# The convolution's last four gate and value outputs computed context first, with its transforms, norm and SiLU placed between the latents' outputs, and the second pointwise product started before the convolution has ended

## The chip, the cores and the metric

One core of one Trainium2 chip runs the whole program. The metric is the device time in microseconds (us) from start to end of one execution; the median of several runs is compared. Before the change three runs took 1692.59, 1693.88 and 1698.11 us, so the median is 1693.88 us.

The core has a matrix engine (PE, whose weight loads are listed as PEld), a vector engine (DVE), an activation engine (ACT), a general engine (POOL) and queues that start transfers (SP). Each engine works through its own rows in a fixed order; a row that waits holds up all rows behind it on that engine.

## The reference

Two streams of 256 tokens with 1024 channels, context and latents, go through two layers. The change lies in the first half of layer 0, the convolution module, which runs once for each stream with the same weights:

```python
def conformer_conv(u, rows, w_pw1, b_pw1, w_dw, b_dw, ln_g, ln_b, w_pw2, b_pw2):
    a = u @ w_pw1 + b_pw1
    a = a[..., :CONV_DIM] * jax.nn.sigmoid(a[..., CONV_DIM:])
    ...
        a = dwconv(a, w_dw)
    ...
    a = jax.nn.silu(layer_norm(a + b_dw, ln_g, ln_b))
    return a @ w_pw2 + b_pw2

y = conformer_conv(modulate(h, sh1, sc1), ...)
h = layer_norm(ALPHA * h + g1 * y, ln1_g[i], ln1_b[i])
```

The scales, shifts and gates (`sh1`, `g1`, `sh2` and so on) come from one product of a small vector with `ada_w` for each stream. After the convolution both streams go through a squared-ReLU MLP, and then through layer 1, which neither the change nor its neighbourhood touches.

## The kernel before, in words

Both streams are held as one array of 512 columns, channels on partitions: columns 0 to 255 (`LO`, s = 0) are the context, columns 256 to 511 (`HI`, s = 1) the latents. All products are float32 split into a high and a low part, so each 128x128 block of weights costs three matmuls (`mm3`: L177, L180, L181). The raw weights come by DMA (`raw_load`), ACT rounds them (`wh`, L154), DVE subtracts (`wl`, L155). Four pairs of `wh`/`wl` are held at a time (`NW`).

**First product (pw1).** It has 16 outputs of 128 channels, alternately gate and value, eight channel blocks f in all. Four of them are computed while the inputs arrive. The other twelve, called outputs 0 to 11 here, follow: 0 to 9 over all 512 columns (`gemm_steps(pw1, range(5), ...)`), 10 and 11 in two halves of 256 columns (`pw1_part`). `pw1_epi` applies sigmoid to the gate (ACT L652), multiplies with the value (DVE L655), transposes the block on PE (L658) and copies it to `A`, tokens on partitions (ACT L659). `pw1_next` also steps the adaLN columns of g1 and sc2 on DVE (`ada0.step`, L379, 1.2 us each and two for a step), and after output 5 scales x by ALPHA and adds gate times bias, 16 DVE operations (L768).

**The convolution.** `spectral(h, tt)` does it by a transform for half h of the channels and 128 tokens tt (0 and 1 are the context, 2 and 3 the latents): forward matmuls (L675 for context, L680 for latents), four multiplications by the taps' transform on DVE (L690, L691), inverse matmuls (L701), the bias (DVE L708) and the statistics (L709). Half 0 runs after output 4, half 1 at the end.

**The end of the convolution.** `token_norm(t0)` turns the statistics of two token tiles into scales by a chain of 13 tiny DVE operations (L714 to L719) and then normalizes four tiles on ACT (L723). `silu(s)` takes one stream's normalized tokens back to channels: for each block f two transposes on PE (L743), a sigmoid and an affine on ACT (L746, L747), a product on DVE (L748), and the split into high and low (L154, L155). Two blocks f share one PSUM bank `ln` of which there are two, and two SBUF buffers `S` are rotated through. `ada_sh` computes the columns of sh2 with the matmuls L319 and the fold L327; it uses the one PSUM bank `fl`.

**Second product (pw2).** `gemm2_steps` runs the context's eight outputs, then the latents' eight; it gives back control after the first ko = 4 outputs together and then after each output, and at each return the loop takes two blocks of `silu(1)`. `pw2_epi` adds to x and feeds the layer norm (`Norm`); after output 7 of a stream it calls `ln1_half`, which finishes the norm and writes the MLP's input: DVE L493, L494 and L516, ACT L515, eight times.

**Order.** The program is recorded in the order of the Python code; a scheduler then places each engine's rows, and rows under `pin[0] = True` keep the order of the code. What stands where is fixed before the program runs.

Of the kernel before, what the change touches and what calls it, by code (L numbers as in the profile page):

```python
# [72 lines left out]
def hybrid_kernel(ctx: ExitStack, tc: tile.TileContext, xT, vecs_d, rows_d, wdw_d, ada0_w, ada_w, adar_w, wg_d, pw1a, pw1, pw2, w1_0, w2_0,  # L73
# [335 lines left out]
    class Norm:  # L409
# [3 lines left out]
        def __init__(self, n, bufs):  # L413
            self.n, self.ts, self.i = n, [], 0
            self.acc, self.k, self.s2 = bufs
# [90 lines left out]
    def norm_pair(make):  # L506

        b = [make() for _ in range(3)]
        return [Norm(C, [t[:, sl] for t in b]) for sl in (LO, HI)]
# [20 lines left out]
    cb = xp.tile([P, 2 * D], F32, tag="hl", name="cb").rearrange("p (s c) -> p s c", s=2)  # L530
    padp = open_pool("pads")
# [205 lines left out]
    def silu(s):  # L737
        for f in range(DT):
# [3 lines left out]
            for i in range(2):  # L742
                nc.tensor.transpose(xn[:, i * P:(i + 1) * P], Y[2 * s + i][f // 4][:, f % 4 * P:f % 4 * P + P], ident)  # L743
# [10 lines left out]
    ada0, ada_sh = AdaRows(0, (2, 4)), Ada(6, 2)  # L754
    gb = con.tile([P, 2, DT], F32, name="gb")

    def pw1_next(m, ps):
# [5 lines left out]
        ada0.step((1, 2, 1, 2, 2, 2, 2, 2, 1, 1)[m])  # L763
        if m == 5:
            for s, sl in HALVES:
                nc.vector.tensor_tensor(gb[:, s, :], ad(0, s, "g1"), VA("b_pw2"), op=ALU.mult)
                for f in range(DT):
                    nc.vector.tensor_scalar(x[f][:, sl], x[f][:, sl], ALPHA, gb[:, s, f:f + 1], op0=ALU.mult, op1=ALU.add)  # L768
# [4 lines left out]
    steps = gemm_steps(pw1, range(5), u, T, pw1_next)  # L773
# [53 lines left out]
    raw = raw_load(pw1[5, 0])  # L827
    wl2 = [split_w(raw[:, m * D:(m + 1) * D]) for m in range(2)]
    ps2 = [psum() for _ in range(2)]

    def pw1_part(m, s, kts=range(DT)):
        sl = HALVES[s][1]
        for kt in kts:
            mm3(ps2[m][:, sl], *kcol(wl2[m], kt), *[t_[:, sl] for t_ in u[kt]], kt == 0, kt == DT - 1)

    def part_epi(m, s):
        pw1_epi(10 + m + KO0, ps2[m], 2 * s, 2 * s + 2)
# [12 lines left out]
    next(sp[0])  # L850
    pw1_part(1, 1, range(4))
    next(sp[1])
    pw1_part(1, 1, range(4, DT))
    for _ in sp[0]:
        pass
    part_epi(1, 1)
    for _ in sp[1]:
        pass
    normed = token_norm(0)
    pre_pw2(1)  # L860
    for tt in (2, 3):
# [3 lines left out]
        for _ in sp1:  # L865
            pass
# [901 lines left out]
```

## Time and profile before

| | |
|---|---|
| median of three runs | 1693.88 us |
| the profiled execution | 1694.68 us |
| its span, first to last instruction | 1693.0 us |
| PE busy | 1661.1 us (98%) |
| DVE busy | 1092.0 us (65%) |
| ACT busy | 745.7 us (44%) |
| end of the convolution and both pw2 passes | 129 to 225 us of the span |

The difference between the profiled execution and its span, 1.68 us, lies ahead of the first and behind the last instruction. A row of the timeline gives the start in us from the start of the span, the duration, the engine, the line, and the tiles that are written and read; the bracket at its end is the idle time ahead of it and what ended that. Durations of back to back rows overlap by about a tenth of a microsecond or more, so what an operation costs in a dense run is read from the distance between two starts.

### The profile page before, as it was taken

The numbers are of one execution on the slowest core, as the hardware profiler recorded it, in microseconds if no ns is written. First come the engines' busy times: TensorE is split into PE (matmuls) and PEld (weight loads), VectorE is DVE, ScalarE is ACT, GpSimd is POOL, SyncE is SP. The second block draws the span as 40 slices with busy tenths as digits, with TensorE's granted clock in tenths as the row PEclk, the third lists the DMA queues.
The fourth block names the chain that finished last, engine by engine and source line by source line (L and its number), as shares of the span: only waits on it lengthen the run. The fifth ranks groups of instructions, "written<-read, shape, count | busy, mean of one in ns | idle before, by whom it ended". The sixth has DMA issues, their size and how long they took to land.

```text
span 1693.0 us, 22721 instructions
## 1 busy us (share of the span) xinstructions
PE 1661.1 (98%) x8853; PEld 1366.3 (81%) x8853; DVE 1092.0 (65%) x1964; ACT 745.7 (44%) x1206; POOL 33.4 (2%) x84
## 2 busy tenths in 40 slices
PE   8998999999999999999999999999999999999998
PEld 5754997888888998876688899888877878888886
DVE  7995897876666776763132543453387786678765
ACT  3322763232324465542232532442376674555652
POOL 0000000000000000000000000000011110000000
PEclk9999999999999999999999999999999999999999
DMA  9534216565554054568653642344355555645651
GB/s 386 210 130 160 102 57 225 199 222 199 199 195 178 26 183 158 190 217 274 239 191 101 219 150 100 104 171 144 119 187 198 187 188 212 242 172 218 240 186 47
DMA packets 60668, 301.60 MB, mean 178 GB/s; under 512 B 6066, under 2 KB 20946, under 8 KB 27152
## 3 DMA queue, kind: packets, MB, share of 16 engines
q1 hardware_dynamic: 42832, 285.44, 46.7%
q10 hardware_dynamic: 17728, 14.70, 2.7%
q8 instruction: 70, 1.15, 0.3%
q14 instruction: 38, 0.31, 0.1%
HBM read 284.37 MB, written 15.75 MB: 177 GB/s over the span
## 4 chain that ended last, share of the span: by engine, by line
PE 91%; DVE 5%; ACT 2%; issue 1%; DMA 1%; POOL 0%; SPq 0%; DVEq 0%; ACTq 0%; POOLq 0%
PE mm L177 17%; PE mm L180 17%; PE mm L181 17%; PE mm L192 4%; PE mm L187 3%; PE mm L185 3%; PE mm L1591 3%; PE mm L186 3%; PE mm L196 2%; PE cv L187 2%; PE cv L186 2%; PE cv L185 2%; PE mm L1592 2%; DVE wl L155 1%; PE fl L812 1%; PE ln L177 1%
## 5 line engine op out<-in xcount | busy, mean ns | idle before, releaser
L155 DVE TENSOR_TENSOR wl<-raw,wh 128x1024 fp32r<-128x1024 f32 x346 | 421.8, 1223 | 306.4 <-ACT wh L154 303.3
L154 ACT CAST wh<-raw 128x1024 fp32r<-128x1024 f32 x346 | 360.4, 1050 | 483.4 <-PE mm L180 286.3
L180 PE MATMUL mm<-u,wh 128*128 128x512 f32 (+1 forms) x848 | 301.8, 357 | 1.0 <-DVE u L525 0.6
L177 PE MATMUL mm<-u,wh 128*128 128x512 f32 (+1 forms) x720 | 253.6, 355 | 3.8 <-DVE E L1014 3.2
L181 PE MATMUL mm<-u,wl 128*128 128x512 f32 (+1 forms) x720 | 250.5, 350 | 0.5 <-DVE wl L155 0.5
L180 PEld LDWEIGHTS mm<-u,wh 128*128 128x128 f32 x848 | 161.1, 190 | 24.5 <-issue 1.8
L177 PEld LDWEIGHTS mm<-u,wh 128*128 128x128 f32 x720 | 136.1, 190 | 28.5 <-issue 5.1
L181 PEld LDWEIGHTS mm<-u,wl 128*128 128x128 f32 x720 | 136.8, 190 | 19.9 <-issue 1.4
L177 PE MATMUL mm<-xm,wh 128*128 128x512 f32 x256 | 102.8, 402 | 0.0
L185 PE MATMUL mm<-wh,xl 128*128 128x512 f32 x256 | 101.3, 397 | 0.7 <-ACT wh L154 0.5
L186 PE MATMUL mm<-wh,xl 128*128 128x512 f32 x256 | 100.4, 392 | 0.6 <-DVE xl L155 0.6
L181 PE MATMUL mm<-xm,wl 128*128 128x512 f32 x256 | 100.3, 392 | 0.0
L187 PE MATMUL mm<-wl,xl 128*128 128x512 f32 x256 | 99.6, 394 | 0.3 <-DVE wl L155 0.2
L379 DVE CUSTOM_DVE_ANT_0 raw<-raw,cb,vecs 128x1024 f32<-128x1024 f32 x64 | 81.6, 1281 | 24.1 <-DMA raw<-adar_w 23.6
L177 PE MATMUL mm<-hid,wh 128*128 128x512 f32 (+1 forms) x256 | 93.2, 364 | 0.0
L180 PE MATMUL mm<-hid,wh 128*128 128x512 f32 (+1 forms) x256 | 92.8, 363 | 0.0
L181 PE MATMUL mm<-hid,wl 128*128 128x512 f32 (+1 forms) x256 | 92.8, 363 | 0.0
L1591 PE MATMUL mm<-x,wh 128*128 128x512 f32 x224 | 78.9, 397 | 0.0
L180 PE MATMUL mm<-qq,wh 128*128 128x272 f32 x256 | 73.9, 289 | 0.0
L181 PE MATMUL mm<-qq,wl 128*128 128x272 f32 x256 | 73.5, 288 | 0.0
L177 PE MATMUL mm<-qq,wh 128*128 128x272 f32 x256 | 73.5, 288 | 0.0
L192 PE MATMUL mm<-u,wh 128*128 128x512 f32 x192 | 68.4, 398 | 0.0
(496 smaller groups left out, 3269.8 us busy)
## 6 DMA issues: line engine op xcount, KB each, us to landing
raw<-w SPq DMA_DIRECT2D x64, 1024.0 KB, 4.9
raw<-adar_w SPq DMA_DIRECT2D x32, 1024.0 KB, 4.9
raw<-wo SPq DMA_DIRECT2D x32, 1024.0 KB, 4.8
raw<-ada_w SPq DMA_DIRECT2D x16, 1024.0 KB, 7.2
raw<-wv SPq DMA_DIRECT2D x16, 1024.0 KB, 5.7
raw<-wqT SPq DMA_DIRECT2D x16, 1024.0 KB, 5.5
raw<-wq SPq DMA_DIRECT2D x16, 1024.0 KB, 4.9
raw<-wk SPq DMA_DIRECT2D x16, 1024.0 KB, 4.9
```

Source lines behind the costliest of these rows:

```text
L154: c = nc.scalar.copy(hi, src)
L155: nc.vector.tensor_tensor(lo, src, hi.bitcast(F32), op=ALU.subtract)
L177: a = nc.tensor.matmul(ps, wh, xh, start=start, stop=False)
L180: nc.tensor.matmul(ps, wh, xl, start=False, stop=False)
L181: nc.tensor.matmul(ps, wl, xh, start=False, stop=stop)
L185: nc.tensor.matmul(ps, xh, wh, start=start, stop=False)
L186: nc.tensor.matmul(ps, xl, wh, start=False, stop=False)
L187: nc.tensor.matmul(ps, xh, wl, start=False, stop=stop)
L192: nc.tensor.matmul(ps, wh, x, start=start, stop=stop)
L196: nc.tensor.matmul(ps[:, :C], wl, x[:, :C], start=False, stop=False)
L379: nc.vector.tensor_tensor_reduce(dump, w, cb[:, s, :], 1.0, vecs[:, o:o + 1], ALU.mult, ALU.add, accum_out=ada[self.l][:, m, s:s + 1])
L1591: a = lambda stop: nc.tensor.matmul(ps, wh, u2[kt], start=kt == 0, stop=stop)
```

## The change

- Outputs 8 and 9 are taken out of the full width loop, so outputs 8 to 11 run in halves: the context's four halves first, then the latents' four.
- The context's transforms of half 1 stand between the latents' outputs 9, 10 and 11; `token_norm(0)` and the first three blocks of `silu(0)` are recorded ahead of the epilogue of output 11.
- The sh2 columns are computed in two parts (`Ada(6, 1)`, `Ada(7, 1)`), and the latents' transforms tt = 2 and 3 come between and behind the rest of `silu(0)`.
- pw2 starts with ko = 3 outputs, ahead of the last inverse transform. `token_norm(2)` follows that. A second `next(steps2)` runs output 3 before the loop that takes the blocks of `silu(1)`.
- The 16 operations that scale x move from DVE to ACT, after output 6; the steps of `ada0` are spread differently.
- The norm's sum `acc` gets a pool of its own, since pw2 now starts before the convolution's pool is closed.

```diff
-    ada0, ada_sh = AdaRows(0, (2, 4)), Ada(6, 2)
+    ada0, ada_sh = AdaRows(0, (2, 4)), [Ada(6, 1), Ada(7, 1)]
...
-        ada0.step((1, 2, 1, 2, 2, 2, 2, 2, 1, 1)[m])
-        if m == 5:
+        ada0.step(1 if m % 2 == 0 else 2)
+        if m == 6:
...
-                    nc.vector.tensor_scalar(x[f][:, sl], x[f][:, sl], ALPHA, gb[:, s, f:f + 1], op0=ALU.mult, op1=ALU.add)
+                    nc.scalar.activation(x[f][:, sl], x[f][:, sl], AF.Identity, scale=ALPHA, bias=gb[:, s, f:f + 1])
...
-    steps = gemm_steps(pw1, range(5), u, T, pw1_next)
+    steps = gemm_steps(pw1, range(4), u, T, pw1_next)
...
-    for m in range(2):
-        pw1_part(m, 0)
-        if m == 0:
-            part_epi(0, 0)
-    pw1_part(0, 1, range(4))
-    part_epi(1, 0)
-    pw1_part(0, 1, range(4, DT))
-    part_epi(0, 1)
+    for m in range(8, 12):
+        pw1_part(m, 0, first4)
+        if m == 10:
+            part_epi(9, 0)
+        pw1_part(m, 0, last4)
+        if m != 9 and m != 11:
+            part_epi(m, 0)
+        ada0.step()
+    pw1_part(8, 1, first4)
+    part_epi(11, 0)
+    pw1_part(8, 1, last4)
+    part_epi(8, 1)
+    sp = [spectral(1, tt, banks=("cv", "fl")) for tt in range(4)]
+    next(sp[0])
+    pw1_part(9, 1)
     pre_pw2(0)
-    sp = [spectral(1, tt, banks=("mm", "fl")) for tt in range(2)]
-    next(sp[0])
-    pw1_part(1, 1, range(4))
     next(sp[1])
-    pw1_part(1, 1, range(4, DT))
-    for _ in sp[0]:
-        pass
-    part_epi(1, 1)
-    for _ in sp[1]:
-        pass
-    normed = token_norm(0)
+    pw1_part(10, 1, first4)
+    part_epi(9, 1)
+    pw1_part(10, 1, last4)
+    part_epi(10, 1)
+    run(sp[0])
+    pw1_part(11, 1, first4)
+    run(sp[1])
+    token_norm(0)
+    pw1_part(11, 1, last4)
+    s0 = silu(0)
+    for _ in range(3):
+        next(s0)
+    part_epi(11, 1)
     pre_pw2(1)
-    for tt in (2, 3):
-        sp1 = spectral(1, tt, normed)
-        next(sp1)
-        ada_sh.mm()
-        for _ in sp1:
-            pass
-    ada_sh.end()
-    pin[0] = False
-    for _ in silu(0):
-        pass
-    token_norm(2)
...
+    ada_sh[0].mm()
+    next(sp[2])
+    run(s0)
+    run(sp[2])
+    ada_sh[0].end()
+    next(sp[3])
...
+    steps2 = gemm2_steps(pw2, range(4), sact, HALVES, pw2_epi, lambda dt: hidden[0](dt), ko=3, pre=pre2)
+    next(steps2)
+    ada_sh[1].mm()
+    run(sp[3])
+    ada_sh[1].end()
+    token_norm(2)
+    pin[0] = False
+    next(steps2)
...
     side = silu(1)
-    for _ in gemm2_steps(pw2, range(4), sact, HALVES, pw2_epi, HD, ko=4, pre=pre2):
+    for _ in steps2:
         for _ in range(Z.nsilu):
             next(side, None)
```

Three places show how rows move. The same code stands 4 to 26 lines further down in the changed file: L756 is the transpose of `silu` that was L743, L759 and L760 are its sigmoid and affine (L746, L747), L761 its product (L748), L668 and L671 the product and the transpose of `pw1_epi` (L655, L658), L693 and L714 the latents' forward and the inverse transforms (L680, L701), L722 and L727 the statistics and their sum (L709, L714), L503 and on the chain of `rsqrt` (L499), L527 is the affine of `ln1_half` on ACT (L515). Numbers in the names tell buffers apart.

The first place is DVE at the context's token statistics. Before, `u_558` and `u_560` are the two tokens tiles of half 1, and `mw` is the small tile of the norm's chain:

```order
L708 TENSOR_TENSOR u_558<-cv_1272,bdw 128x512
L155 TENSOR_TENSOR wl_1319<-raw_1312,wh_1318 128x1024
L709 BN_STATS bst<-u_558 128x6
L708 TENSOR_TENSOR u_560<-cv_1284,bdw 128x512
L714 BN_AGGR mv_1291<-bst 128x2
L709 BN_STATS bst<-u_560 128x6
L714 BN_AGGR mv_1291<-bst 128x2
L499 TENSOR_SCALAR mw_1294<-mv_1291 128x2
L500 TENSOR_SCALAR mw_1294<-mw_1294 128x2
L502 TENSOR_TENSOR mw_1294<-mw_1294 128x2
```

In the change the same tiles are `u_561` and `u_563`; `E_1148` is the block of output 11 of the latents, `wl_1407` the low part of pw2's fourth weight block:

```order
L721 TENSOR_TENSOR u_563<-cv_1326,bdw 128x512
L727 BN_AGGR mv_1333<-bst 128x2
L722 BN_STATS bst<-u_563 128x6
L668 SCALAR_TENSOR_TENSOR E_1148<-mm_1313,vecs,E_1148 128x256
L727 BN_AGGR mv_1333<-bst 128x2
L503 TENSOR_SCALAR mw_1336<-mv_1333 128x2
L155 TENSOR_TENSOR wl_1407<-raw_1400,wh_1406 128x1024
L504 TENSOR_SCALAR mw_1336<-mw_1336 128x2
L506 TENSOR_TENSOR mw_1336<-mw_1336 128x2
L507 SCALAR_TENSOR_TENSOR mw_1336<-mw_1336 128x2
```

The product that ends output 11 and the split of a weight block now stand inside the chain of the context's norm; before, one weight split stood ahead of the statistics and nothing inside the chain.

The second place is PE behind that norm. Before, the context's first transposes come behind the forward transform of tile 2 and half of the sh2 product, and write two banks, `ln_1393` and `ln_1412`, in turn:

```order
L680 MATMUL mm_1323<-A,tab 128x512
L680 MATMUL mm_1322<-A,tab 128x512
L319 MATMUL fl_1334<-raw_1335,cs 32x512 x4
L319 MATMUL fl_1334<-raw_1337,cs 32x512 x4
L743 MATMUL ln_1393<-ident,u_557 128x128
L743 MATMUL ln_1412<-ident,u_557 128x128
L743 MATMUL ln_1393<-ident,u_559 128x128
L743 MATMUL ln_1412<-ident,u_559 128x128
```

In the change they come straight behind the last matmuls of output 11 (`mm_1313`):

```order
L181 MATMUL mm_1313<-u_508,wl_1116 128x256
L756 MATMUL ln_1366<-ident,u_560 128x128
L756 MATMUL ln_1366<-ident,u_562 128x128
L756 MATMUL ln_1366<-ident,u_560 128x128
L756 MATMUL ln_1366<-ident,u_562 128x128
L756 MATMUL ln_1385<-ident,u_560 128x128
L756 MATMUL ln_1385<-ident,u_562 128x128
L671 MATMUL ln_1396<-ident,E_1148 128x128 x2
L319 MATMUL fl_1410<-raw_1411,cs 32x512 x4
L319 MATMUL fl_1410<-raw_1413,cs 32x512 x4
L693 MATMUL fl_1426<-A,tab 128x512
L693 MATMUL cv_1425<-A,tab 128x512
```

Four transposes now write one bank (`ln_1366`) in a row, the transposes of output 11 (`ln_1396`) stand behind six of them, and the sh2 product and the forward transform of tile 2, which stood ahead of the transposes, stand behind them all. Behind these rows come the other transposes, the fold, the inverse transform of tile 2, and only then pw2's first row.

The third place is ACT at the latents' `silu` and the context's `ln1_half`. Before, `S_1809` and `S_1818` are the last two blocks of the latents, and L475 is the square root of the context's layer norm:

```order
L746 ACTIVATE S_1809<-ln_1806,vecs 128x256
L747 ACTIVATE S_1809<-ln_1806,vecs 128x256
L746 ACTIVATE S_1818<-ln_1806,vecs 128x256
L747 ACTIVATE S_1818<-ln_1806,vecs 128x256
L453 ACTIVATE L_1803<-x_415 128x256
L154 CAST u_1813<-S_1809 128x256
L154 CAST u_1822<-S_1818 128x256
L154 CAST wh_2294<-raw_2292 128x1024
L453 ACTIVATE L_1861<-x_467 128x256
L154 CAST wh_2298<-raw_2292 128x1024
L475 ACT_TABLE_LOAD
L475 ACTIVATE lc_1872<-lc_1872,eps 128x2
```

In the change the sixth block of the latents (`S_1867`) is the last one ahead of that square root (L479), and the context's affine operations begin:

```order
L759 ACTIVATE S_1867<-ln_1855,vecs 128x256
L760 ACTIVATE S_1867<-ln_1855,vecs 128x256
L154 CAST u_1871<-S_1867 128x256
L479 ACT_TABLE_LOAD
L479 ACTIVATE lc_1921<-lc_1921,eps 128x2
L527 ACTIVATE u_1945<-x_146,cb_1936,ca_1935 128x256
L527 ACTIVATE S_1947<-x_146,cb_1936,ca_1935 128x256
L527 ACTIVATE S_1955<-x_180,cb_1936,ca_1935 128x256
```

The seventh and eighth block (`S_2010`, `S_2019`) stand behind the last of the 16 affine operations:

```order
L527 ACTIVATE u_1993<-x_418,cb_1936,ca_1935 128x256
L527 ACTIVATE u_2001<-x_470,cb_1936,ca_1935 128x256
L527 ACTIVATE S_2003<-x_470,cb_1936,ca_1935 128x256
L759 ACT_TABLE_LOAD
L759 ACTIVATE S_2010<-ln_2007,vecs 128x256
L760 ACTIVATE S_2010<-ln_2007,vecs 128x256
L154 CAST u_2014<-S_2010 128x256
L759 ACTIVATE S_2019<-ln_2007,vecs 128x256
L760 ACTIVATE S_2019<-ln_2007,vecs 128x256
L154 CAST u_2023<-S_2019 128x256
```

The code records `ln1_half` at output 7, and with output 3 taken ahead of the loop only six of the eight blocks are recorded by then, where before all eight were. On PE the matmuls that read `u_2014` and `u_2023` stand ahead of output 3 of the latents and of all that follows.

More of the change, by code (lines that the diff above doesn't have):

```diff
@@ L826, in hybrid_kernel, with pw1_part @@
         pass
[L827 to L831, printed above, removed]
+    late_w = {}
+    def pw1_part(m, s, kts=range(DT), bank=None):
         sl = HALVES[s][1]
+        if kts[0] == 0:
+            late_p[m, s] = psum()
+        if m not in late_w:
+            raw = raw_load(pw1[m // 2, 0])
+            for i in range(2):
+                late_w[m + i] = split_w(raw[:, i * D:(i + 1) * D])
@@ L846, in hybrid_kernel, with run @@
-    pw1_part(0, 1, range(4, DT))
-    part_epi(0, 1)
+        pw1_epi(m + KO0, late_p[m, s], 2 * s, 2 * s + 2)
+    def run(g):
+        for _ in g:
+            pass
+    first4, last4 = range(4), range(4, DT)
+    pin[0] = True
+    for m in range(8, 12):
[8 more added lines that the diff above has]
+    part_epi(11, 0)
```

41 lines of the change are left out of this document (28 added, 13 removed).

## The prediction

> **What bounds the kernel now.** Read first the busy time and the chain of work that ended last, on the page of the profile:
>
> ```profile
> PE 1661.1 (98%) x8853; PEld 1366.3 (81%) x8853; DVE 1092.0 (65%) x1964; ACT 745.7 (44%) x1206; POOL 33.4 (2%) x84
> ...
> PE 91%; DVE 5%; ACT 2%; issue 1%; DMA 1%; POOL 0%; SPq 0%; DVEq 0%; ACTq 0%; POOLq 0%
> ```
>
> PE works 98% of the span and carries 91% of the chain. DVE (65%) and ACT (44%) set the end only where PE waits, so the change is worth what it does to PE's idle time and clock. Then the timeline of PE where the change lies (start, duration, operation; the bracket is the idle time ahead and what ended it):
>
> ```profile
> 105.86 0.50 PE L181 MATMUL mm<-u,wl 128*128 128x512 f32 x1 [0.47 <-DVE wl L155]
> ...
> 130.58 0.63 PE L658 MATMUL ln<-ident,E 128*128 128x128 f32 x4 [0.94 <-ACT wh L154]
> ...
> 152.33 1.13 PE L680 MATMUL mm<-A,tab 64*128 64x512 f32 x4
> 153.39 1.92 PE L319 MATMUL fl<-raw,cs 128*32 128x512 f32 x16
> 158.37 1.39 PE L743 MATMUL ln<-ident,u 128*128 128x128 f32 x4 [3.06 <-ACT u L723]
> 159.69 3.68 PE L701 MATMUL cv<-F,tab 128*64 128x512 f32 x8
> ...
> 164.89 1.93 PE L319 MATMUL fl<-raw,cs 128*32 128x512 f32 x16
> 166.75 0.44 PE L743 MATMUL ln<-ident,u 128*128 128x128 f32 x2
> 167.53 1.94 PE L701 MATMUL cv<-F,tab 128*64 128x512 f32 x8 [0.34 <-DVE F L690]
> 169.40 1.05 PE L327 MATMUL fl<-fold,F 128*128 128x4 f32 x8
> ...
> 171.64 0.38 PE L180 MATMUL mm<-u,wh 128*128 128x256 f32 x1 [0.45 <-DVE u L155]
> ```
>
> PE waits 0.94, 3.06, 0.34 and 0.45 us at the convolution's end, and 0.47 earlier. The large wait ends when ACT has normalized the context. The table of stretches (width, busy time of PE, PEld, DVE, ACT and POOL, granted clock, DMA) shows what comes with it:
>
> ```profile
> 156.00:160.00 4.00, 1.61 (x6) 0.87 (x8) 3.61 (x12) 2.49 (x4) 0.00 (x0) 0.70 0.98 373
> 160.00:164.00 4.00, 4.00 (x10) 0.98 (x8) 1.00 (x2) 1.34 (x3) 0.00 (x0) 0.50 0.59 246
> 164.00:168.00 4.00, 3.66 (x24) 0.81 (x22) 3.12 (x7) 0.78 (x2) 0.00 (x0) 0.95 0.21 35
> ```
>
> The clock is at half for 0.60 x 4.0 = 2.4, 4.0 and 0.10 x 4.0 = 0.4 us, 6.8 in all, about 157.6 to 164.4. PE has work again from 158.37, so 6.0 us run at half and 3.0 are lost. The most that a perfect cover of this stage could win is thus 4.8 us of waits and 3.0 of clock, under 0.5%.
>
> **The change part by part**, against the profiled 1694.68.
>
> *x is scaled on ACT.* What leaves DVE, what ACT pays, and where:
>
> ```profile
> L768 DVE TENSOR_SCALAR x<-x,gb 128x256 f32<-128x256 f32 x16 | 4.7, 345 | 0.0
> ...
> L515 ACT ACTIVATE u<-x,cb,ca 128x256 fp32r<-128x256 f32 x16 | 9.4, 590 | 1.3 <-DVE x L494 1.3
> ...
> 105.42 0.58 ACT L659 COPY A<-ln 128x512 f32<-128x512 f32 x1 [23.63 <-PE ln L658]
> ```
>
> 16 operations of 0.345, busy 4.7 us with their overlaps, leave DVE. The nearest ACT rows, an affine operation of the same size, take 0.59; 16 are 9.4 us, beside ACT's 23.63 idle us ahead of 105.42. No row shows this very operation on ACT; the ends are 0 (covered) and +9.4 (all in PE's path). I take 0, by the idle row. DVE, freed, ends the weight split earlier: the wait of 0.47 goes, **−0.5**. Should the cover fail, the copy at 105.42 is the next on ACT that something waits for. The end of 9.4 is left out of the range, since 9.4 fits twice into 23.63.
>
> *Outputs 8 and 9 in halves.* 48 matmuls of 512 columns become 96 of 256:
>
> ```profile
> 126.99 0.39 PE L180 MATMUL mm<-u,wh 128*128 128x512 f32 x1
> 127.22 0.39 PE L181 MATMUL mm<-u,wl 128*128 128x512 f32 x1
> ...
> 171.86 0.28 PE L181 MATMUL mm<-u,wl 128*128 128x256 f32 x1
> 171.98 0.28 PE L180 MATMUL mm<-u,wh 128*128 128x256 f32 x1
> ```
>
> Starts lie 0.23 apart at 512 and 0.12 at 256: 96 x 0.12 − 48 x 0.23 = **+0.5**. SP issues the same weight loads in nearly the same order; DMA in the quoted stretches is at most 0.98 full in one and 0.21 in another, and none of PE's waits above ends on a DMA. I take 0 for the loads. The step of `ada0` and the separate pool for `acc` add no instruction; 0.
>
> *Waits that go.* The four waits from 130.58 to 171.64 belong to an order that no longer exists: −4.8, and with the clock −3.0, **−7.8**. What is late in their place comes now.
>
> *Transposes right behind their producers.* Output 7's transposes, and later L491, stand with no matmuls between product and transpose. Neither wait is in the trace; the ends are 0 and twice the 0.94 of the 130.58 row. I take 0.9 each, **+1.8**, near that row.
>
> *The first hole.* The rows of DVE in the statistics chain, and ACT's and the epilogue's:
>
> ```profile
> 137.08 0.48 DVE L655 SCALAR_TENSOR_TENSOR E<-mm,vecs,E 128x256 f32<-128x256 f32 x1 [5.32 <-PE mm L181]
> ...
> 151.52 1.22 DVE L155 TENSOR_TENSOR wl<-raw,wh 128x1024 fp32r<-128x1024 f32 x1
> ...
> 154.94 0.17 DVE L499 TENSOR_SCALAR mw<-mv 128x2 f32<-128x2 f32 x1
> 155.14 0.17 DVE L500 TENSOR_SCALAR mw<-mw 128x2 int32<-128x2 int32 x1
> ...
> 157.30 0.17 DVE L719 TENSOR_SCALAR mw<-mw 128x2 f32<-128x2 f32 x1
> ...
> 157.51 2.93 ACT L723 ACTIVATE u<-u,mw 128x512 f32<-128x512 f32 x4 [6.78 <-DVE mw L719]
> ...
> L746 ACT ACTIVATE S<-ln,vecs 128x256 f32<-128x256 f32 x16 | 9.1, 567 | 8.7 <-PE ln L743 7.6 <-DVE u L155 1.0
> L747 ACT ACTIVATE S<-ln,vecs 128x256 f32<-128x256 f32 x16 | 9.0, 562 | 0.0
> ...
> L154 ACT CAST u<-S 128x256 fp32r<-128x256 f32 x16 | 6.4, 404 | 0.8 <-DVE S L748 0.7
> ```
>
> (157.51 is four normalizations; the grouped rows give 0.57, 0.56 and 0.40.) Count from the end of output 11's last matmul. Before, the norm chain ran while PE had the forward transform of tile 2 and the sh2 product, from 152.33 (the first of these) to 155.3. In the change both stand behind the transposes, and the transposes behind output 11. Only its last 12 matmuls (12 x 0.12 = 1.4 us) cover the chain, and those end with the inverse transform's bias and statistics still running on DVE. Then:
> - the product of output 11 (0.48 with 0.1 of hand-over) stands in the chain: 0.6
> - the second tile's aggregate and first chain operation: 0.4, at 1.0
> - the weight split (1.22): at 2.2
> - 12 chain operations at 155.14 − 154.94 = 0.20: 2.4, at 4.6
> - ACT's four normalizations (2.9): at 7.5
> - block 0: transposes, sigmoid and affine 0.47 + 0.47 by starts: at 8.5
> - block 1 writes the same bank, so its transposes wait for that affine: sigmoid, cast, affine, 1.3, at 9.8
> - two more transposes, output 11's transposes and the L319 product: 1.0, at 10.8
>
> PE works about 1.0 of these 10.8 us: **+9.8**. The weight split could slip out of the chain (its cast waits for PE's release of the slot): −1.2.
>
> *Behind the hole.* PE has the sh2 product, forward and inverse transform of tile 2, the fold and the rest of the transposes: 1.9 (153.39) + 1.1 (152.33) + 1.9 (167.53) + 1.1 (169.40) and ten transposes, 1.6 (0.44 for two at 166.75, less the overlap of 0.1) = 7.6 us of work. Every second step of them waits for ACT or DVE: the sh2 product at half clock costs +1.8 (3.7, as the transform at 159.69 cost against the 1.94 at 167.53); the copy ahead of the bank `fl` 0.65; the multiplications of two transforms ahead of the inverse 0.6; transposes of block 5 0.7 and of block 7 2.1 behind ACT: **+5.9**. No row shows these waits; the ends are 0 and twice that. I take the sum, since each waits for operations of measured length with nothing else on PE between.
>
> *The second hole.* pw2 runs the context's outputs, then the latents' first three. ACT's order puts the last two blocks of `silu(1)` behind the context's whole `ln1_half`. Price:
>
> ```profile
> 206.53 1.28 ACT L475 ACT_TABLE_LOAD   x1
> 207.83 0.29 ACT L475 ACTIVATE lc<-lc,eps 128x2 f32<-128x2 f32 x1
> ...
> 216.20 0.41 DVE L494 TENSOR_TENSOR x<-x,ln 128x256 f32<-128x256 f32 x1
> 216.53 0.41 DVE L493 TENSOR_TENSOR x<-x,ln 128x256 f32<-128x256 f32 x1
> ...
> L515 ACT ACTIVATE S<-x,cb,ca 128x256 f32<-128x256 f32 x16 | 9.4, 591 | 0.0
> ```
>
> PE does L491, then has the latents' blocks 6 and 7 as its next input. From there: DVE's 24 operations (three for each of eight blocks) at 216.53 − 216.20 = 0.33: 22 until the last affine may start, 7.3; two affines at 0.49 spacing, 1.0; the table load 1.28 (the next operation starts at 207.83, 0.02 after it ends); sigmoid and affine 0.9; product, cast and hand-overs 1.0. That is 11.5, less 0.4 of transposes: **+11.1**. Before, all eight blocks were recorded ahead of `ln1_half`, and the fill for L491's DVE work were latents' outputs. Everything that could fill PE, output 3 of the latents and on, is now queued behind the matmuls that read block 6.
>
> *The clock behind the second hole* falls as it did behind the 3.06 wait: 6.0 us at half, **+3.0**.
>
> Sum: −0.5 + 0.5 − 7.8 + 1.8 + 9.8 + 5.9 + 11.1 + 3.0 = +23.8, so 1718.5. The profiled execution lies 0.8 above the median (1694.68 − 1693.88), so the runs should have their median at **1717.7**. Nothing behind gives it back: pw2 ends at 225.31 and from there PE runs dense:
>
> ```profile
> 225.10 0.28 PE L181 MATMUL mm<-u,hid 128*128 128x256 f32 x1
> 225.31 1.05 PE L319 MATMUL fl<-raw,cs 128*32 128x512 f32 x2
> ```
>
> It will end near 225.3 + 23.8 = 249.1.
>
> [...]
>
> **The rivals.**
> - *The chain is covered* (the other side): the norm of the context ends within the matmuls around it, and blocks 6 and 7 come out ahead of ln1_half's work. Then only −7.8 − 0.5 + 0.5 remain, 1686.1 on the median's scale. It decides at whether output 11's last matmuls outlast the chain: 12 cover 1.4 us where the chain needs 4.6 on DVE alone. For it speaks that DVE is relieved and pw2's weights are early; against it the three order places. 4%.
> - *Only the first hole*: output 3's fill or a faster norm lets blocks 6 and 7 through. Without 11.1 and 3.0: 1703.6. Against it: ACT's order is fixed and the sigmoid stands behind the 16th affine. 9%.
> - *Partly covered, no change*: holes of about the size of what goes, 7.8, 1694. This is also the time if the new order does not do what it says and pw2's early start only fills the last inverse transform. 4%.
> - *The clock stays full*: −1.8 − 3.0, 1712.9; inside the forecast's range.
>
> **How the numbers follow.** The forecast (both holes) has 83%. Its bounds: low without the half clock (−4.8), with the split out of the chain (−1.2) and the unseen waits at 0 (−4.1, what of the 5.9 is not clock, and −1.8), 1705.8; high with those waits doubled (+4.1 and +1.8) and the cold stretch after the second hole doubled (+3.0), 1726.6. The single hole lies just below, so the range is 1703.5 to 1726.6; what is left out are the two cases at 1694 and below and the tails, below 2 in 10. A difference of 0.3% (5.1 us) is about what a measurement of this kernel can tell from no change: faster 4%, the same 4%, slower 92%.
>
> **What the changed profile would show.** PE idle ahead of L756 with ACT's normalization (L736) as releaser, and ahead of output 11's transposes with ACT's affine; clock 0.5 in that stretch. A second idle of some 11 us ahead of an L177 that reads block 6, released by ACT, with an ACT table load at L759 just before; DVE busy with L497, L498 and L528 during it. pw2's end near 249. The early part, to 130, the same within 1 us. Wrong would be: no idle above 3 us behind L491 (then the single hole), L756's wait under 3 us (then the chain is covered), or idle that is released by a DMA.

## The result and the profile after

The change makes the kernel slower: 1722.65 us median of four runs (1721.37 to 1726.29) against 1693.24 for the kernel before (four runs, 1692.24 to 1698.11), a ratio of 1.0163 with a 95% interval of 1.0148 to 1.0179. The profiled execution has a span of 1722.2 us, 29.2 longer than the 1693.0 of before.

The busy times and the chain, from the page of the profile of the changed kernel:

```profile
PE 1672.5 (97%) x8909; PEld 1376.1 (80%) x8909; DVE 1090.1 (63%) x1951; ACT 755.7 (44%) x1226; POOL 33.5 (2%) x84
...
PE 89%; DVE 5%; ACT 3%; issue 1%; DMA 1%; POOL 0%; SPq 0%; DVEq 0%; ACTq 0%; POOLq 0%
```

PE's share of the chain fell from 91% to 89% and ACT's rose from 2% to 3%. PE's busy time grew by 11.4 us (1672.5 − 1661.1). The change adds 56 matmuls (8909 − 8853): 48 come from the halves, priced at 0.5 us, and eight from a second fold, since the sh2 columns are now computed in two parts and each part is folded by eight matmuls of the trace. That fold takes 1.05 us (the row at 194.73 below; the kernel before folds once, at 169.40). Most of the rest is work at half clock, some 9 us by estimate: PE is busy for 16.9, 3.6 and 3.4 us of the change's half clock and for 6.0 us of that before, and half of the difference of 17.9 is lost. The sh2 product shows the rate: its 16 rows take 3.64 us at a clock of 0.50 (164.89 below) and took 1.93 in a stretch at 0.95 (164.89 before). What PE waited for, summed over the execution (total, times, longest):

```profile
PE ln L756 <- ACT S L760: 13.0, 2, 11.2
PE ln L756 <- ACT u L736: 5.6, 2, 5.4
...
PE ln L491 <- DVE L L486: 1.3, 1, 1.3
```

The transposes of SiLU now wait 18.6 us for ACT, where before they waited 3.06. The timeline of PE gives their places:

```profile
116.64 0.55 PE L671 MATMUL ln<-ident,E 128*128 128x128 f32 x3 [1.02 <-DVE E L668]
...
159.15 0.47 PE L756 MATMUL ln<-ident,u 128*128 128x128 f32 x1 [5.36 <-ACT u L736]
159.85 0.48 PE L756 MATMUL ln<-ident,u 128*128 128x128 f32 x1 [0.23 <-ACT u L736]
...
162.16 1.11 PE L756 MATMUL ln<-ident,u 128*128 128x128 f32 x4 [1.84 <-ACT S L760]
...
164.27 0.69 PE L671 MATMUL ln<-ident,E 128*128 128x128 f32 x2 [0.99 <-ACT S L760]
164.89 3.64 PE L319 MATMUL fl<-raw,cs 128*32 128x512 f32 x16
...
194.73 1.05 PE L327 MATMUL fl<-fold,F 128*128 128x2 f32 x8
...
221.98 1.10 PE L491 MATMUL ln<-L,ones 128*128 128x512 f32 x2 [1.25 <-DVE L L486]
...
234.44 0.69 PE L756 MATMUL ln<-ident,u 128*128 128x128 f32 x2 [11.15 <-ACT S L760]
```

The two holes are there, the first between 153.6 and 165 in four pieces, 8.4 us, the second 11.15 us in one. The table of stretches (PE busy, and the granted clock as the third number from the end) shows what the first costs beside its idle time:

```profile
156.00:160.00 4.00, 0.62 (x2) 0.33 (x2) 1.86 (x13) 1.72 (x3) 0.00 (x0) 0.55 0.70 248
160.00:164.00 4.00, 1.44 (x5) 0.74 (x5) 0.64 (x2) 3.22 (x7) 0.00 (x0) 0.50 0.04 14
164.00:168.00 4.00, 3.73 (x18) 0.89 (x18) 1.81 (x5) 2.13 (x6) 0.00 (x0) 0.50 0.13 20
168.00:172.00 4.00, 3.10 (x11) 1.10 (x8) 1.18 (x2) 0.00 (x0) 0.00 (x0) 0.50 0.86 311
172.00:176.00 4.00, 3.70 (x16) 2.97 (x15) 3.43 (x9) 3.04 (x7) 0.00 (x0) 0.50 0.47 195
176.00:180.00 4.00, 4.00 (x8) 0.93 (x9) 2.28 (x6) 2.63 (x7) 0.00 (x0) 0.50 0.00 0
180.00:184.00 4.00, 4.00 (x23) 2.34 (x20) 3.69 (x8) 1.16 (x3) 0.00 (x0) 0.96 0.00 0
...
236.00:240.00 4.00, 4.00 (x25) 3.92 (x25) 2.34 (x6) 2.38 (x4) 0.00 (x0) 0.71 0.00 0
```

In this execution the clock stays at half from about 156.4 (0.45 x 2 x 4 = 3.6 us of the stretch that ends at 160), in the idle time, to about 180.3 (0.04 x 2 x 4 = 0.3), through a stage in which PE is busy for most of the time from 164 on.

Ahead of the second hole, ACT's rows (start, duration, operation) read as the order had them:

```profile
224.02 0.60 ACT L527 ACTIVATE u<-x,cb,ca 128x256 fp32r<-128x256 f32 x1 [3.31 <-DVE x L498]
...
232.07 1.28 ACT L759 ACT_TABLE_LOAD   x1
233.37 0.56 ACT L759 ACTIVATE S<-ln,vecs 128x256 f32<-128x256 f32 x1
233.83 0.56 ACT L760 ACTIVATE S<-ln,vecs 128x256 f32<-128x256 f32 x1
```

The affine operations of `ln1_half` run from 224.02 to 232.07 with a table load behind them, and only then comes the sigmoid of block 6. PE's row at 234.44 is the pair of transposes of block 7, which wait for the affine of block 6 in the same bank (the blocks are counted from 0, so these are the last two).

In the chain of the context's norm on DVE, the product of output 11 and a weight split stand where the order put them:

```profile
153.89 0.48 DVE L668 SCALAR_TENSOR_TENSOR E<-mm,vecs,E 128x256 f32<-128x256 f32 x1 [0.26 <-PE mm L181]
...
154.52 0.17 DVE L503 TENSOR_SCALAR mw<-mv 128x2 f32<-128x2 f32 x1
154.78 1.22 DVE L155 TENSOR_TENSOR wl<-raw,wh 128x1024 fp32r<-128x1024 f32 x1
155.92 0.16 DVE L504 TENSOR_SCALAR mw<-mw 128x2 int32<-128x2 int32 x1
```

154.78 is the split, 1.14 us to the next start, inside a chain that releases ACT at 158.28.

### The profile page after: what moved, and what is told of

It is laid out like the page before. It is cut to its first block, busy times and chain, and to the rows that moved or that the text cites. A ratio compares the mean times of both kernels' runs of the same rounds, so it can differ in the third digit from the quotient of the medians.

```text
span 1722.2 us, 22859 instructions
## 1 busy us (share of the span) xinstructions
PE 1672.5 (97%) x8909; PEld 1376.1 (80%) x8909; DVE 1090.1 (63%) x1951; ACT 755.7 (44%) x1226; POOL 33.5 (2%) x84
## 4 chain that ended last, share of the span: by engine, by line
PE 89%; DVE 5%; ACT 3%; issue 1%; DMA 1%; POOL 0%; SPq 0%; DVEq 0%; ACTq 0%; POOLq 0%
PE mm L177 17%; PE mm L180 16%; PE mm L181 16%; PE mm L192 3%; PE mm L187 3%; PE mm L185 3%; PE mm L1634 3%; PE mm L186 3%; PE mm L196 2%; PE cv L186 2%; PE cv L187 2%; PE cv L185 2%; PE mm L1635 2%; DVE wl L155 1%; PE fl L319 1%
## 5 line engine op out<-in xcount | busy, mean ns | idle before, releaser
L180 PE MATMUL mm<-u,wh 128*128 128x512 f32 (+1 forms) x872 | 307.9, 354 | 0.6 <-DVE u L537 0.6
L177 PE MATMUL mm<-u,wh 128*128 128x512 f32 (+1 forms) x744 | 261.6, 353 | 3.6 <-DVE E L1057 3.2
L181 PE MATMUL mm<-u,wl 128*128 128x512 f32 (+1 forms) x744 | 257.8, 347 | 0.0
L180 PEld LDWEIGHTS mm<-u,wh 128*128 128x128 f32 x872 | 167.3, 192 | 23.1 <-issue 1.5
L177 PEld LDWEIGHTS mm<-u,wh 128*128 128x128 f32 x744 | 142.6, 193 | 30.2 <-issue 6.9
L181 PEld LDWEIGHTS mm<-u,wl 128*128 128x128 f32 x744 | 142.8, 192 | 18.3 <-issue 1.2
L177 PE MATMUL mm<-xm,wh 128*128 128x512 f32 x256 | 102.8, 402 | 0.0
L177 PE MATMUL mm<-hid,wh 128*128 128x512 f32 (+1 forms) x256 | 93.3, 365 | 0.0
L177 PE MATMUL mm<-qq,wh 128*128 128x272 f32 x256 | 73.5, 289 | 0.0
```

The lines of the kernel that those rows point to most:

```text
L177: a = nc.tensor.matmul(ps, wh, xh, start=start, stop=False)
L180: nc.tensor.matmul(ps, wh, xl, start=False, stop=False)
L181: nc.tensor.matmul(ps, wl, xh, start=False, stop=stop)
```

## The experiments

Each is compared with runs of the kernel before on its own chip; the ratio to those is given, and a difference in us is the difference of ratios times 1694. The changed kernel's ratio is 1.0163.

**e_blocks: two blocks of SiLU earlier.**

```diff
     side = silu(1)
+    for _ in range(Z.nsilu):
+        next(side, None)
     for _ in steps2:
```

> Two blocks of the latents' SiLU are recorded behind output 3 too, so all eight stand ahead of the context's ln1_half; all else as changed. Theory (the second hole comes from the order on ACT): the idle of 11.15 us ahead of the transposes and the 2.0 us lost to half clock behind it go, with about 1 us of small waits in their place: 1722.7 - 12 = about 1710.5, and PE's idle between 222 and 236 under 2 us. Rival (PE has nothing else to do there in any order, since DVE's 24 operations hold up what follows): the hole moves behind block 8, 1717 to 1723.

1711.9 us, ratio 1.0094 (1.0076 to 1.0112): 11.7 us less than the change. The place of the hole, on PE:

```profile
215.18 0.50 PE L177 MATMUL mm<-u,wh 128*128 128x256 f32 x2 [0.54 <-ACT u L154]
...
225.00 0.62 PE L177 MATMUL mm<-u,wh 128*128 128x256 f32 x3 [0.37 <-ACT u L154]
226.15 1.10 PE L491 MATMUL ln<-L,ones 128*128 128x512 f32 x2
```

The largest wait between 210 and 232 is 0.54 us, and L491 (226.15) has no wait. The rival falls: the hole is gone and does not appear behind block 8. The second hole comes from the place of the two blocks behind the context's affine operations. The edit moves their rows on PE and DVE as well, but what PE waited for was ACT's affine.

**e_norm: transposes put back behind other work.**

```diff
-    token_norm(0)
     pw1_part(11, 1, last4)
-    s0 = silu(0)
-    for _ in range(3):
-        next(s0)
     part_epi(11, 1)
-    pre_pw2(1)
+    token_norm(0)
     ada_sh[0].mm()
     next(sp[2])
+    pre_pw2(1)
+    s0 = silu(0)
     run(s0)
```

> Output 11 and its epilogue, then the sh2 product and the forward transform of tile 2 stand ahead of the context's transposes, as they did before the change; all else as changed. Theory (the first hole comes from the place of the transposes): of the 8.4 us of idle between 153 and 165 some 3 remain, as the 3.06 of the kernel before, and half clock lasts about 6 us instead of 17: -5.4 and -5, about 1712. Rival (the SiLU chain on ACT, some 10 us for eight blocks, is the bound and only changes its place): 1718 to 1723, with the idle spread over the later transposes.

1721.41 us, ratio 1.0150 (1.0133 to 1.0167): 2.2 us less, within what the intervals allow for no difference. The theory as put falls, and the rival (1718 to 1723, with the idle time spread over the later transposes) is what happened. The wait ahead of the first transposes shrinks to 0.68, but later transposes wait:

```profile
165.53 1.11 PE L756 MATMUL ln<-ident,u 128*128 128x128 f32 x4 [2.09 <-ACT S L760]
...
168.34 1.12 PE L756 MATMUL ln<-ident,u 128*128 128x128 f32 x4 [1.70 <-ACT S L760]
...
171.16 0.69 PE L756 MATMUL ln<-ident,u 128*128 128x128 f32 x2 [1.70 <-ACT S L760]
```

2.09, 1.70 and 1.70 us, each released by ACT's affine: the idle time has moved from ahead of the first transposes to between the later ones.

**e_warm: filler in the first hole.**

```diff
     pw1_part(11, 1, last4)
+    hot = psum()
+    for i in range(12):
+        pe(nc.tensor.matmul(hot, ident, A[:, 0, 0:512], start=True, stop=True))
     s0 = silu(0)
```

> Twelve extra matmuls of 128 x 512 on unused data (nothing reads the result) stand between output 11 and the context's first transposes, 12 x 0.43 = 5.1 us inside an idle of 5.36; all else as changed. Theory (the clock falls in the idle time and comes back only after dense work): the clock stays full until about 159, falls later or not at all, and of the 8.4 us lost at half clock up to 181 between 4 and 8 come back: 1714.5 to 1719. Rival (the sparse rows behind the hole, transposes and narrow products with waits between them, lower the clock by themselves): half clock from about 162 to 181 as now, 1721 to 1724.

1722.12 us, ratio 1.0156 (1.0138 to 1.0174). The filler was sized wrongly. Rows of its size lie 0.43 apart in the kernel before (L675, two from 79.96 to 80.83), but each of the twelve runs as two operations in the trace, and they take 10.46 us, not 5.1, so the first transposes come late:

```profile
151.41 10.46 PE L892 MATMUL mm<-A,ident 128*128 128x512 f32 x24
161.70 0.38 PE L756 MATMUL ln<-ident,u 128*128 128x128 f32 x2
```

From the end of output 11 (151.41 here, 153.6 in the change) to pw2's first matmul it is 182.52 − 151.41 = 31.1 us, against 182.19 − 153.6 = 28.6 in the changed kernel. The clock did stay up during the filler, and fell again later, in two pieces of 3.4 and 6.8 us:

```profile
156.00:160.00 4.00, 4.00 (x11) 1.72 (x10) 0.03 (x1) 2.94 (x4) 0.00 (x0) 1.00 0.49 205
...
164.00:168.00 4.00, 2.94 (x14) 0.89 (x18) 2.04 (x5) 2.92 (x8) 0.00 (x0) 0.62 0.01 2
...
176.00:180.00 4.00, 3.26 (x10) 1.06 (x10) 2.05 (x6) 2.40 (x6) 0.00 (x0) 0.50 0.02 4
```

So the clock fell in the idle time of the change (0.55 from 156 to 160) and stayed full here (1.00) while the filler ran. That it comes back only after dense work, as the theory had it, no run shows. From the first transposes to pw2 the stage takes 20.8 us (161.70 to 182.52) where it took 23.0 (159.15 to 182.19), and nothing is won in the end, since the filler cost more.

What the half clock itself costs behind the hole is shown better by e_blocks, whose rows on PE are the same there. From the sh2 product to pw2's first matmul, first in the change, then in e_blocks:

```profile
164.89:182.19 17.30, 16.10 (x51) 6.12 (x50) 9.95 (x22) 8.16 (x19) 0.00 (x0) 0.55 0.34 122
165.97:183.16 17.19, 13.82 (x52) 4.58 (x51) 10.81 (x23) 8.12 (x19) 0.00 (x0) 0.71 0.34 122
```

At 0.55 some 15.6 us of the stretch ran at half clock (0.45 x 2 x 17.30), at 0.71 some 10.0, and the length is the same, 17.3 and 17.2 us (16.9 in e_xdve at 0.72 and in e_warm at 0.72). Where PE is faster it waits longer for ACT and DVE: e_blocks has a wait of 1.69 us ahead of the last transposes, the change none there. So in this stage the clock is not what sets the time.

**e_both: the diffs of e_blocks and e_norm together.**

> The edits of e_blocks and e_norm together. If the two holes are independent, and the first is bound by the chain of SiLU on ACT (what e_norm showed): 1722.7 - 10.8 - 1.2 = about 1710.5. Rival (e_norm's gain was hidden by the second hole): 1700 to 1705.

1707.87 us, ratio 1.0076 (1.0062 to 1.0090), between the two expectations: 14.7 us less than the change, where the single edits gave 11.7 and 2.2. So the two losses add up.

**e_unpin: e_both, with pw2's rows between the transposes.**

```diff
     pre_pw2(1)
+    pin[0] = False
     s0 = silu(0)
     run(s0)
```

> e_both, and the rows from the context's transposes on are free to be ordered among pw2's, so that pw2's matmuls stand between them, as in the kernel before. Theory (behind the first hole PE waits for ACT because nothing but transposes stands there): the waits of 2.09, 1.70 and 1.70 us that e_norm had ahead of transposes go, and most of the half clock: 1701 to 1705. Rival (ACT needs its 10 us for eight blocks in any order, and PE waits for the last of them): 1708 to 1712.

1699.81 us, ratio 1.0032 (1.0021 to 1.0043), 7.5 us less than e_both. The three waits ahead of transposes are gone, and the clock is full in the stretch:

```profile
164.00:168.00 4.00, 4.00 (x17) 1.53 (x16) 1.58 (x4) 2.36 (x6) 0.00 (x0) 1.00 0.60 254
168.00:172.00 4.00, 3.89 (x30) 3.38 (x28) 3.79 (x9) 3.06 (x7) 0.00 (x0) 1.00 0.00 0
```

This is a little better than the theory had it (1701 to 1705). So most of the first loss that these edits take away comes from the pinned order, in which pw2's matmuls stand behind the transposes of all eight blocks. The transposes go at ACT's pace (waits of 2.09, 1.70 and 1.70 us in e_norm), and PE has little else. In the kernel before and here, pw2's matmuls of one block stand between the transposes of the next ones. The edit frees the transforms and the fold in that stretch as well, and these were not separated. The kernel is still 5.4 us above the one before: the 56 added matmuls are about 1.5 of it, and where the rest comes from is not shown.

**e_xdve: x scaled on DVE again.**

```diff
-                    nc.scalar.activation(x[f][:, sl], x[f][:, sl], AF.Identity, scale=ALPHA, bias=gb[:, s, f:f + 1])
+                    nc.vector.tensor_scalar(x[f][:, sl], x[f][:, sl], ALPHA, gb[:, s, f:f + 1], op0=ALU.mult, op1=ALU.add)
```

> The 16 operations that scale x go back from ACT to DVE; all else as changed. Theory (ACT does them for nothing, and DVE is the bound of that stretch): the wait of 1.02 us ahead of the transposes of output 7 grows by what DVE has more to do, 4.7 us at most, 1723 to 1728. Rival (DVE had room, or ACT's scaling costs something): 1720 to 1723.

1727.5 us, ratio 1.0188 (1.0167 to 1.0208): 4.2 us more than the change. The profile shows a part of it:

```profile
116.72 0.66 PE L671 MATMUL ln<-ident,E 128*128 128x128 f32 x4 [1.77 <-DVE E L668]
...
118.92 1.12 PE L799 MATMUL ln<-F,tab 31*128 31x512 f32 x2 [0.49 <-ACT A L672]
```

1.77 and 0.49 us where the change has 1.02. These rows speak for moving the scaling; the intervals of the two kernels overlap, so the times alone do not show it.

**e_bact: the kernel before with x scaled on ACT alone** (the two lines of e_xdve the other way round, behind output 5).

> The kernel before, with x scaled on ACT alone. Theory: ACT does it in idle time and the wait of 0.47 goes, perhaps 0.83 more ahead of the forward transform at 84.4: 1693 to 1694.5. Rival (the scaling is in the way of something on ACT): above 1695.5.

1694.01 us, ratio 0.9990 (0.9981 to 0.9998): faster by about 1.7 us, as far as it can be told. The part that was to cost nothing costs nothing.

**e_early: the context's transforms earlier, the latter part as before.** Outputs 8 to 11 as in the change, then

```diff
+    run(sp[0])
     pw1_part(10, 1, last4)
     part_epi(10, 1)
-    run(sp[0])
-    pw1_part(11, 1, first4)
     run(sp[1])
-    token_norm(0)
-    pw1_part(11, 1, last4)
...
+    normed = token_norm(0)
+    pw1_part(11, 1)
+    part_epi(11, 1)
+    pre_pw2(1)
+    for tt in (2, 3):
+        sp1 = spectral(1, tt, normed)
+        next(sp1)
+        ada_sh.mm()
+        run(sp1)
+    ada_sh.end()
+    pin[0] = False
+    run(silu(0))
```

with `Ada(6, 2)` and ko = 4 as before.

> The latter part as in the kernel before (ko = 4, all four transforms ahead of SiLU, both sh2 columns in one, no pinned rows behind), but outputs 8 to 11 context first, both inverse transforms of the context ahead of the latents' output 11; x scaled on ACT. Theory (what the change wanted needs cover behind the statistics, here 24 matmuls of output 11, two forward transforms and the sh2 product, some 8 us against a chain of 5 to 6): the wait of 3.06 and the 3.0 lost at half clock go: 1694.5 - 6 = 1687 to 1691. Rival (another wait takes the place, a late load for sh2 or ACT's SiLU): 1693 to 1698.

1694.4 us, ratio 0.9990 (0.9981 to 0.9999). It is not the 1687 to 1691 of the theory, but what the rival said. The 3.06 is gone and the clock is full (1.00) from 150 to 188. The waits of that place are now

```profile
156.10 0.44 PE L671 MATMUL ln<-ident,E 128*128 128x128 f32 x2 [0.66 <-DVE E L668]
...
166.28 1.06 PE L319 MATMUL fl<-raw,cs 128*32 128x512 f32 x8 [1.53 <-DMA raw<-ada_w]
```

and three smaller ones; the largest, 1.53, is for a load of sh2's weights. At 116 there are 1.23 us of wait and, in the profiled execution, 6.8 us of half clock behind them. In that execution most of what was won behind is lost there.

**e_steps, e_steps2, e_cols, e_last: the wait at 116.** All four start from e_early. e_steps spreads the adaLN columns to later outputs, e_steps2 issues `pre_pw2(1)` behind the first `ada_sh.mm()` as well; the lines of the spread are:

```diff
-        ada0.step(1 if m % 2 == 0 else 2)
+        ada0.step((1, 2, 1, 2, 1, 1, 1, 0)[m])
...
-        ada0.step()
+        ada0.step((2, 2, 2, 1)[m - 8])
```

> e_early with four of the adaLN columns that DVE steps through during outputs 4 to 7 put off to outputs 8 to 10, where DVE is idle most of the time. Theory (the wait of 1.23 us ahead of the transposes of output 7 comes from DVE's columns, and the 6.8 us of half clock that follow come from that wait): the wait goes, the clock stays full between 116 and 126, and the median falls by 1.2 and by what the half clock cost in the mean, up to 3.4: from 1694.4 to 1689.5 to 1693. Rival (the half clock comes from the sparse rows there, the transposes and the four narrow products for the taps, with or without a wait): the wait goes but half clock still shows in the profile, 1693 to 1694.5.

> e_steps, and the load of pw2's second weights is issued behind the first pair of loads for sh2 instead of ahead of them. Theory (the wait of 1.53 us ahead of the second sh2 product is the rotation of the three load buffers): that wait shrinks below 0.5, 1 us less than e_steps. Rival (the load of pw2's weights then comes late for the first rows of pw2): a wait of over 1 us ahead of pw2's third output, no faster than e_steps.

e_steps 1696.13 us, ratio 1.0007 (0.9998 to 1.0015); e_steps2 1692.98, ratio 0.9989 (0.9980 to 0.9999). e_steps lies above both its expectations. The wait at 116 stayed (1.46 in both), since the scheduler placed seven column operations ahead of the product on DVE where e_early has six; the first theory was not tried by these. The wait for sh2's load was 1.53 in e_early, 1.16 in e_steps and 1.02 in e_steps2, less of a gain than expected. e_cols is e_steps2 with the columns held back until the product of output 7 is done, by an ordering edge on DVE:

```diff
+        with tc.issue_after(hold["e7"].ins):
+            ada0.step((2, 2, 2, 1)[m - 8])
```

> e_steps2 with the adaLN columns of outputs 8 to 11 held back on DVE until the product of output 7 is done (in e_steps and e_steps2 they were still ordered ahead of it, and the wait stayed at 1.46). Theory: the wait ahead of the transposes of output 7 goes, and with it the half clock that some executions show at 118 to 126: 1693.0 - 1.5 - up to 1.7 in the mean = 1689.8 to 1691.5, and no half clock before 150 in the profile. Rival (the half clock there comes from the sparse rows alone): the wait goes, half clock can still show, 1691 to 1693.

1696.7 us, ratio 1.0009 (1.0000 to 1.0018). Neither expectation: the wait shrinks to 0.91 and does not go, and others appear.

```profile
116.22 0.66 PE L671 MATMUL ln<-ident,E 128*128 128x128 f32 x4 [0.91 <-DVE E L668]
...
126.17 0.39 PE L181 MATMUL mm<-u,wl 128*128 128x256 f32 x1 [1.06 <-DVE wl L155]
...
128.91 0.44 PE L671 MATMUL ln<-ident,E 128*128 128x128 f32 x2 [1.28 <-DVE E L668]
```

DVE has the same columns to do before 136, and what is pushed past one product stands ahead of the next. What is left of the wait at 116 is answered by DVE's row of that product in e_cols, beside the transposes of output 7 in the kernel before:

```profile
115.42 0.75 DVE L668 SCALAR_TENSOR_TENSOR E<-mm,vecs,E 128x512 f32<-128x512 f32 x1 [9.30 <-PE mm L181]
```

```profile
117.85 0.60 PE L658 MATMUL ln<-ident,E 128*128 128x128 f32 x4
```

In e_cols DVE had been idle for 9.30 us and took up the product 0.11 us after output 7's last matmul ended (116.22 − 0.91 = 115.31). The transposes start 0.80 us after the product does, and nothing else stands on PE in between. So 0.9 us of wait belong to the order on PE, whatever DVE has to do. In the kernel before, matmuls of output 8 run on PE while DVE does the product, from 116.68, and the transposes (117.85) have no wait. DVE's load adds only how late the product starts: 0.22 us in the change, 0.21 in e_last, 0.43 in e_early, 0.66 in e_steps, 0.97 in e_xdve; with the 0.80 this gives the waits of 1.02, 1.01, 1.23, 1.46 and 1.77.

e_last is e_steps2 with the spread of the kernel before and the scaling on ACT after output 5:

```diff
-        ada0.step((1, 2, 1, 2, 1, 1, 1, 0)[m])
-        if m == 6:
+        ada0.step((1, 2, 1, 2, 2, 2, 2, 2)[m])
+        if m == 5:
...
-        ada0.step((2, 2, 2, 1)[m - 8])
+        ada0.step((1, 1, 0, 0)[m - 8])
```

> e_steps2's latter part, with the adaLN columns spread as in the kernel before and x scaled on ACT behind output 5. Theory (the wait ahead of the transposes of output 7 comes from the other spread of columns and from scaling later; e_bact, with this spread, had no such wait): the wait goes, the norm's cover stays, 1689 to 1691.5. Rival (the wait only moves to the next product, as in e_cols, since DVE has the same columns to do before 136): 1692.5 to 1696.

1692.67 us, ratio 0.9982 (0.9973 to 0.9991): the fastest of all, some 3 us under the kernel before. Its wait at 116 is still 1.01, so the theory was wrong on the cause: of that wait DVE's load is only the 0.21, and the rest stands with any spread of the columns.

## Why the prediction was right, and where its terms were off

It said 1717.7 in a range of 1703.5 to 1726.6; the median is 1722.65. The likeliest case, two holes from the order, is what happened. What it would take to close the first hole, and what the clock does, came out otherwise in part.

- **The second hole**, +11.1: measured 11.15 in one wait, with ACT's affine operations, table load and sigmoid in the order named. PE stops one step earlier than the prediction said: not at the L177 that reads block 6, but at the transposes of block 7, which need the bank of block 6. The table load costs 1.28 and the next operation starts 0.02 us after it, as in the kernel before. e_blocks removes the hole, and 11.7 us go with it.
- **The clock behind it**, +3.0: half clock lasts to about 238.3 (0.29 x 4 x 2 = 2.3 us of the stretch from 236). PE has work from 234.44 but for a wait of 0.28, some 3.6 us of it at half, so 1.8 were lost. The prediction took the 6.0 us behind the 3.06 wait as the size, and that was one execution's: behind a wait of 3.06 in the same place e_bact has 3.4 us of half clock, where the kernel before has 6.8.
- **The first hole**, +9.8: from the end of output 11 (153.6) to the sh2 product (164.89) it is 11.3 us instead of 10.8, of which 8.4 are idle. The product and the split in the chain, the four normalizations and the shared bank all appear as steps. As a cause, though, the place of the first transposes is a small part of it: e_norm takes that away and wins 2.2, because the idle time comes back ahead of the later transposes.
- **Behind the hole**, +5.9: this is the term that was mis-sized most. From 164.89 to pw2's first matmul (182.19) it is 17.3 us where the terms made 7.6 + 5.9 = 13.5. Of the difference, 1.1 is the forward transform of tile 3, which the new order also puts ahead of pw2 and which the 7.6 left out; that is work and no loss. So 8.6 us are lost, 2.7 more than priced. The prediction charged half clock for the sh2 product alone, and the trace has it up to about 180.3, but the clock is not the reason: e_blocks has the same rows with 5.6 us less of half clock and takes as long. The prediction priced this stage rightly as a string of hand-overs between PE, ACT and DVE with nothing else on PE. The pinned order that makes it so is what e_unpin takes away, together with the half clock: 7.5 us.
- **The early part**, −0.5 + 0.5 and no change "within 1 us" up to 130: wrong. The wait of 0.47 goes, as said, and so does the 0.94 at 130.58. But in the profiled execution 3.4 us run at half clock behind the new wait at 116.64 (1.7 lost), and no step of the prediction had this.
- **Waits behind their producers**, +1.8: output 7's transposes wait 1.02 (116.64) and L491 waits 1.25, together 2.3. The reason is the one given, no matmuls between product and transposes, as e_cols shows for the first of them.
- **The sh2 columns in two parts**: the sum has no term for them. The second fold is 1.05 us of work.
- **Nothing gives it back**: the last epilogue of pw2 (L917) starts at 255.3 instead of 227.3, 28 us later, and the span is 29.2 longer.

The two rivals that went the other way fail on the same rows: PE idle of 8.4 us in the first hole (so the chain was not covered) and 11.15 in the second. The sum was off by 29.2 − 23.8 = 5.4: +2.7 behind the hole, +1.7 for the clock of the early part, +1.0 for the second fold, +0.5 in the first hole, +0.5 for the waits behind their producers, −1.2 for the clock of the second hole. That makes 5.2; 0.2 is left over. That the total comes so near is in part luck: the last of these goes against the others, and the half clock differs from one execution to the next (the mean clock of the change's four runs is 0.985, 0.990, 0.987 and 0.986).

## What to carry to other kernels

A chain moved earlier gains nothing unless rows that do not need it stand behind its start on the engine that waits (PE was idle for 8.4 us in the first hole): count them in microseconds, and count the chain. Work on two engines that hand blocks back and forth (transposes on one, activations on the other) needs independent rows between the blocks on the faster engine; pinning the order of the blocks takes these away (e_unpin, 7.5 us). When a generator is advanced once more ahead of its loop, look at what the loop does at each step, since here two blocks fell behind a whole layer norm. And before a wait is put down to a busy engine, look at when that engine takes up the row: the wait at 116 was 0.91 us in e_cols, where DVE had been idle for 9.30.

## What the runs showed of the hardware

The pieces of half clock that were seen between 100 and 260 us of these profiles are 3.4 us long or whole multiples of that. Behind the waits at 116, in stretches of 2 us (granted clock third from the end), first e_both, then e_norm, whose rows on PE and DVE stand in the same order there:

```profile
116.00:118.00 2.00, 1.74 (x7) 1.09 (x8) 2.00 (x3) 0.61 (x2) 0.00 (x0) 0.96 0.85 356
118.00:120.00 2.00, 2.00 (x4) 0.50 (x4) 1.96 (x5) 0.97 (x2) 0.00 (x0) 0.50 0.95 311
120.00:122.00 2.00, 2.00 (x11) 2.00 (x11) 1.97 (x3) 0.41 (x1) 0.00 (x0) 0.50 0.75 315
122.00:124.00 2.00, 2.00 (x11) 2.00 (x11) 0.71 (x6) 0.00 (x0) 0.00 (x0) 0.50 0.21 49
124.00:126.00 2.00, 2.00 (x17) 2.00 (x16) 0.00 (x0) 0.48 (x1) 0.00 (x0) 0.84 0.93 385
```

```profile
118.00:120.00 2.00, 2.00 (x15) 1.57 (x14) 1.96 (x5) 1.05 (x2) 0.00 (x0) 1.00 0.92 295
```

A clock of 0.50 is counted as half clock all the time, one of 0.84 as a third of the time. e_both sums to 0.16 + 6.0 + 0.64 = 6.8 us behind a wait of 1.09, e_norm to nothing behind one of 1.18. Six kernels have the same code up to this place. The change has 3.4 us of half clock here, e_blocks, e_both and e_unpin 6.8, e_norm and e_warm none. So the same rows show 0, 3.4 or 6.8 us of half clock from one profile to another. The length of the wait does not tell them apart: it is 1.02 us in the change (3.4), in e_blocks and e_unpin (6.8) and in e_warm (none), and behind the 1.46 of e_steps there is none either.

The longer stretches are whole multiples as well, by the same sum: of the pieces of half clock that the tables of stretches show between 100 and 260 us, in the profiles of fourteen kernels, none is off a multiple of 3.41 (23.9 / 7) by more than 0.1. It is 23.9 us (seven) in the first hole of the change and 13.6 (four) at its second, as in e_norm, e_warm and e_xdve. In the first stage e_blocks and e_xdve have 10.2 (three) and then 6.8 (two). The kernel before has 6.8 behind its 3.06 and e_bact 3.4 behind the same 3.06. What sets the length of a piece, and what makes the clock fall, is not shown. Single profiles of these kernels should be compared with this in mind: at 116 two of them with the same order differ by 6.8 us of half clock, which is some 3 us of time by estimate, since PE is busy there and half of it is lost.
